# Sixteen more tokens by fetched expert rows, and a dense pass for 400 tokens in place of 416

## The chip, the core and the metric

The kernel runs on one core of a Trainium2 chip. The metric is the device time of one execution in microseconds (us), taken as the median of several runs. All data are fp32; products that need precision are made of three matmuls of split operands (high times high, high times low, low times high).

In the profile, PE is TensorE (its matmuls) and PEld its weight loads, DVE is VectorE, ACT is ScalarE, POOL is GpSimd, SP is SyncE, which issues most DMAs.

## The reference

One decoder layer for 576 tokens (512 of a prompt, 64 of eight running sequences): a mixer of windowed attention and a recurrent branch, then PEER, a layer of 16,384 experts, of which every token picks 16 in each of 8 heads. The change concerns PEER alone:

```python
def one(hc):
    c = hc.shape[0]
    q = (hc @ w_pq).reshape(c, PEER_HEADS, 2, D_KEY // 2)
    s = jnp.einsum('nhcd,hckd->nhck', q, sub_keys)
    sv, si = lax.top_k(s, PEER_TOPK)
    cand = (sv[:, :, 0, :, None] + sv[:, :, 1, None, :]).reshape(c, PEER_HEADS, -1)
    cid = (si[:, :, 0, :, None] * N_KEYS + si[:, :, 1, None, :]).reshape(c, PEER_HEADS, -1)
    best, pos = lax.top_k(cand, PEER_TOPK)
    eid = jnp.take_along_axis(cid, pos, axis=-1)
    g = jax.nn.softmax(best, axis=-1)
    act = jax.nn.gelu(jnp.einsum('nd,nhkd->nhk', hc, peer_u[eid]))
    return jnp.einsum('nhk,nhkd->nd', g * act, peer_v[eid])
```

`peer_u` and `peer_v` have 16,384 rows of 2,048 numbers each.

## The kernel before

Two ways of doing PEER run side by side.

**Dense.** The first `DEN` = 416 tokens are multiplied with all experts. `u_parts` (L741) makes the scores of one chunk of 128 experts: 16 blocks of 128 features, three matmuls each, with the weights loaded as the stationary operand and 416 token columns streamed (`mm3`, L96 to L99, tile `sps`). There are 128 chunks. The gelu of the scores goes to `e`; the first 40 chunks are put by in DRAM (`Ed`). The routing weights G of each token for each expert are built ahead (loop at L980 to L1008): for each token one product of two one-hot tiles (`pgg`, L1000), copied to a staging tile `stg` (ScalarE, L1002) and written to DRAM (`Gd`) in 13 groups of `GRP` = 32 tokens. Then come 16 groups of 8 chunks (`v_group`, L1159): `w_chunk` (L1147) multiplies `e` with G (tile `gs`, loaded from `Gd` by `load_g` and, for the next group, in pieces by L1170) and splits it, and 16 blocks of 24 matmuls make the output features (tile `po`), again with 416 columns; VectorE adds each block to `acc` (L1174). Between the groups run the score chunks of the next one. Weights arrive in pieces of 256 KB (`piece`, L75): a DMA issued on SP, a rounding on ScalarE (`phi`), a subtraction on VectorE (`plo`).

**Fetched.** The last 128 tokens lie one on each partition, and for each of their 128 expert slots the u row and the v row are fetched with an indirect DMA, in halves of 1,024 numbers for all 128 partitions at once, 512 KB a fetch (`fetch`, L1064, GpSimd's queue). VectorE makes the dot product (`gather_u`, L1072) or adds the scaled row (`gather_v`, L1078). 32 more tokens (`SPR`) are spread over four partitions each, so that each partition takes two heads of one token: 32 further slots. Their normalised rows are laid out by `spread_rows` (L765) through TensorE transposes (`ptx`) and DRAM (`hsd`), their routing results are put in place by small DMAs (`es`, L925), and at the end `spread_sum` (L1136) folds the four partitions of each token with 16 fp32 matmuls (`psum`). These are 160 slots, 640 fetches. `pace` (L1108) spreads them over the work: the dense part counts 464 units of 24 matmuls, and after unit 20 each unit may issue its share of the fetches, behind that unit's last split in VectorE's order.

Which experts the 128 tokens use is found by `gather_top` (L1031), eight heads of two small products (`psg`, "slot products" here) with top-16 searches on VectorE; one step of it is taken after each of the 16 blocks of the first V group.

A tile framework orders the instructions of each engine ahead of time from data dependencies and its own estimates; each engine then runs its queue in that order. `with tc.issue_after(ins)` makes the instructions that the block creates on the engine of `ins` stand behind it.

Of the kernel before, what the change touches and what calls it, by code (L numbers as in the profile page):

```python
# [8 lines left out]
F32 = mybir.dt.float32  # L9
# [17 lines left out]
DEN = 416  # L27
SPR = DQ - DEN
GRP = 32
BT = 8  # L30
NGRP = DEN // GRP
# [16 lines left out]
def tile_hymba_peer_step(ctx: ExitStack, tc: tile.TileContext, a, o, dbg=None):  # L48
# [47 lines left out]
    def mm3(out, sh, sl, mh, ml, first, last):  # L96
        pe.matmul(out, lhsT=sh, rhs=mh, start=first, stop=False)  # L97
        pe.matmul(out, lhsT=sh, rhs=ml, start=False, stop=False)  # L98
        pe.matmul(out, lhsT=sl, rhs=mh, start=False, stop=last)  # L99
# [27 lines left out]
    Gd = gd_pool.tile([NSG, P, NGRP, 8, GRP], F32, name="Gd")  # L127
# [517 lines left out]
    rt = per.tile([P, 5], F32, name="rt")  # L645
    es3 = per.tile([P, 3, SPR], F32, name="es3")
# [74 lines left out]
    def ffn_rstd():  # L721
# [10 lines left out]
        rsq(rt, pn[:, 0:5], 1.0 / D)  # L732
# [30 lines left out]
    hsd = gd_pool.tile([P, D], F32, name="hsd")  # L763

    def spread_rows(g4, pl):  # L765

        q = slice(g4 * 4, g4 * 4 + 4)
        t = pl.tile([P, 4, 4, SPR], F32, tag="sx", name="sx", bufs=2)
        dve.tensor_tensor(t, acc[:, q, None, DEN:].to_broadcast([P, 4, 4, SPR]),
                          gffn[:, q, None, None].to_broadcast([P, 4, 4, SPR]), op=ALU.mult)  # L770
# [4 lines left out]
        act.activation(r, pt.rearrange("p j n -> p (j n)"), AF.Copy, scale=rt[:, 4:5])  # L775
        sp.dma_start(hsd[:, g4 * 512:g4 * 512 + 512], r)
# [72 lines left out]
    with tc.tile_pool(name="tq", bufs=1) as tq:  # L849
# [35 lines left out]
        for h in range(8):  # L885
# [53 lines left out]
    with tc.tile_pool(name="gb", bufs=1) as gbp, tc.tile_pool(name="psg", bufs=2, space=PSUM) as psg:  # L939
# [37 lines left out]
        for r in range(NGRP):  # L977
# [6 lines left out]
            if g == 2 and t < 3:  # L984
                nxt = prep(t + 1)
# [327 lines left out]
```

## Time and profile before

| | us |
|---|---|
| median of 3 runs | 3421.17 (3417.39 to 3424.73) |
| the profiled execution | 3426.56 |
| its span, first to last instruction | 3424.8 |
| mean granted TensorE clock | 0.992 |
| busy PE / DVE / ACT / POOL | 3354.9 / 2535.3 / 1238.8 / 1229.3 |
| moved by DMA | 770.74 MB, 225 GB/s over the span |
| of it by fetches (GpSimd's queue) | 335.59 MB |

Busy times are sums over stages with different limits, and consecutive matmuls overlap in the profile, so TensorE's busy time is no measure of how fast it is fed. The table by stretch, the distance between matmul starts and the waits say more.

### The profile page before, as it was taken

To read this page: it belongs to the slowest core of one execution; us is meant where nothing else is said; L and a number is where in the kernel's file an instruction comes from. 1 tells how busy PE (TensorE), PEld (TensorE's weight loads), DVE (VectorE), ACT (ScalarE), POOL (GpSimd) and SP (SyncE) were. 2 spreads that over 40 slices of the span, in tenths; PEclk is the share of its full clock that TensorE was granted. 3 is DMA by queue.
4 is the path that set the end of the run, shared out by engine and by line. 5 is a ranking of instruction groups with operands and counts; after the bars stand their busy time and mean duration, and the time that the engine had idled before them with its cause. 6 is when DMAs were issued, how large, how long until landed. Compare 5 with 4: busy or idle time off the path is not lost.

```text
span 3424.8 us, 52637 instructions
## 1 busy us (share of the span) xinstructions
PE 3354.9 (98%) x18611; PEld 3220.6 (94%) x18611; DVE 2535.3 (74%) x4765; ACT 1238.8 (36%) x2127; POOL 1229.3 (36%) x1174
## 2 busy tenths in 40 slices
PE   9999999999999997999999999999999999999999
PEld 7887888889899997899999999999999999999999
DVE  5476655444759887888888887888878888888885
ACT  4245544333334443333333332333333333333332
POOL 6562231123642001434343333334333433443331
PEclk9999999999999999999999999999999999999999
DMA  4221223343334665789998888888888888988885
GB/s 146 81 63 55 67 63 111 99 142 110 92 97 137 204 223 183 284 290 332 334 315 291 300 297 300 300 294 298 292 307 303 287 309 295 316 306 289 307 290 193
DMA packets 364297, 770.74 MB, mean 225 GB/s; under 512 B 41184, under 2 KB 115552, under 8 KB 363744
## 3 DMA queue, kind: packets, MB, share of 16 engines
q1 hardware_dynamic: 266112, 423.26, 36.5%
q0 software_dynamic: 92160, 335.59, 29.2%
q10 hardware_dynamic: 5760, 8.52, 0.7%
q8 instruction: 147, 2.41, 0.3%
q14 instruction: 118, 0.97, 0.1%
HBM read 724.03 MB, written 45.11 MB: 225 GB/s over the span
## 4 chain that ended last, share of the span: by engine, by line
PE 88%; DVE 5%; DMA 2%; POOL 2%; issue 1%; ACT 1%; SPq 0%; ACTq 0%; DVEq 0%; POOLq 0%
PE po L99 11%; PE po L97 11%; PE po L98 11%; PE sps L99 10%; PE sps L97 10%; PE sps L98 10%; PE pgg L1000 3%; PE pd L99 2%; PE pd L98 2%; PE pd L97 2%; PE zp L97 2%; PE zp L98 1%; PE zp L99 1%; PE pdq L99 1%; PE mm L97 1%
## 5 line engine op out<-in xcount | busy, mean ns | idle before, releaser
L92 ACT ACTIVATE phi<-raw 128x512 fp32r<-128x512 f32 x1200 | 756.9, 632 | 1640.0 <-PE po L98 698.8
L93 DVE TENSOR_TENSOR plo<-raw,phi 128x512 fp32r<-128x512 f32 x1132 | 795.4, 704 | 283.9 <-ACT phi L92 266.1
L97 PE MATMUL po<-wth,phi 128*128 128x416 f32 x2048 | 719.7, 352 | 6.3 <-ACT wth L70 4.3
L99 PE MATMUL po<-wth,plo 128*128 128x416 f32 x2048 | 724.5, 354 | 0.0
L98 PE MATMUL po<-wtl,phi 128*128 128x416 f32 x2048 | 716.8, 350 | 0.6 <-DVE wtl L71 0.6
L1066 POOL DMA_INDIRECT row<-in_v,idx x320 | 396.1, 1238 | 605.0 <-DVE xg L1078 375.7
L1066 POOL DMA_INDIRECT row<-in_u,idx x320 | 388.6, 1214 | 589.8 <-DVE au L1072 465.3
L99 PE MATMUL sps<-uha,plo 128*128 128x416 f32 x1536 | 539.5, 351 | 5.9 <-DVE plo L93 3.3
L97 PE MATMUL sps<-uha,phi 128*128 128x416 f32 x1536 | 537.9, 350 | 1.2 <-DVE e L753 1.2
L98 PE MATMUL sps<-ula,phi 128*128 128x416 f32 x1536 | 537.5, 350 | 0.0
L97 PEld LDWEIGHTS po<-wth,phi 128*128 128x128 f32 x2048 | 385.6, 188 | 11.1 <-ACT wth L70 5.3
L98 PEld LDWEIGHTS po<-wtl,phi 128*128 128x128 f32 x2048 | 386.3, 189 | 8.2 <-DVE wtl L71 1.3
L99 PEld LDWEIGHTS po<-wth,plo 128*128 128x128 f32 x2048 | 385.5, 188 | 2.6
L1078 DVE SCALAR_TENSOR_TENSOR xg<-row,gg,xg 128x1024 f32<-128x1024 f32 x256 | 321.6, 1280 | 0.3
L1072 DVE CUSTOM_DVE_ANT_0 row<-row,hg 128x1024 f32<-128x1024 f32 x256 | 307.1, 1220 | 7.2 <-DMA row<-in_u,idx 7.2
L99 PEld LDWEIGHTS sps<-uha,plo 128*128 128x128 f32 x1536 | 289.0, 188 | 8.9 <-DVE plo L93 5.6
L97 PEld LDWEIGHTS sps<-uha,phi 128*128 128x128 f32 x1536 | 289.2, 188 | 1.7 <-ACT scs L860 1.4
L98 PEld LDWEIGHTS sps<-ula,phi 128*128 128x128 f32 x1536 | 289.0, 188 | 0.2
L1174 DVE TENSOR_TENSOR acc<-po,acc 128x416 f32<-128x416 f32 x256 | 150.8, 590 | 158.6 <-PE po L99 157.2
L99 PE MATMUL sps<-uhb,plo 128*128 128x416 f32 x512 | 181.3, 354 | 5.0 <-DVE plo L93 5.0
L98 PE MATMUL sps<-ulb,phi 128*128 128x416 f32 x512 | 180.2, 352 | 0.0
L97 PE MATMUL sps<-uhb,phi 128*128 128x416 f32 x512 | 180.1, 352 | 0.0
(427 smaller groups left out, 5316.9 us busy)
## 6 DMA issues: line engine op xcount, KB each, us to landing
raw<-in_uT SPq DMA_DIRECT2D x512, 256.0 KB
raw<-in_vL SPq DMA_DIRECT2D x512, 256.0 KB
Gd<-stg SPq DMA_DIRECT2D x13, 2048.0 KB
gs<-Gd SPq DMA_DIRECT2D x196, 128.0 KB
raw<-in_wlru SPq DMA_DIRECT2D x64, 256.0 KB
raw<-in_wout SPq DMA_DIRECT2D x64, 256.0 KB
raw<-in_wpq SPq DMA_DIRECT2D x64, 256.0 KB
raw<-in_wqkv SPq DMA_DIRECT2D x48, 256.0 KB
```

The lines of the kernel that those rows point to most:

```text
L92: act.activation(hi, raw, AF.Copy)
L93: ins = (pool if on_pool else dve).tensor_tensor(lo, raw, hi.bitcast(F32), op=ALU.subtract)
L97: pe.matmul(out, lhsT=sh, rhs=mh, start=first, stop=False)
L98: pe.matmul(out, lhsT=sh, rhs=ml, start=False, stop=False)
L99: pe.matmul(out, lhsT=sl, rhs=mh, start=False, stop=last)
L1000: pe.matmul(pg[:, k], lhsT=ohB[:, k], rhs=ohA[:, k].rearrange("p a b -> p (a b)"), start=True, stop=True)
L1066: pool.indirect_dma_start(out=r, out_offset=None, in_=uv[w], in_offset=bass.IndirectOffsetOnAxis(ap=idx2[:, half, e:e + 1], axis=0))
L1072: dve.tensor_tensor_reduce(r, r, rows[0][:, half * 1024:half * 1024 + 1024], 1.0, 0.0, ALU.mult, ALU.add, au[:, half, e:e + 1])
L1078: dve.scalar_tensor_tensor(xs, r, gg[:, e:e + 1], xs, op0=ALU.mult, op1=ALU.add)
L1174: dve.tensor_tensor(acc[:, b, 0:DEN], po, acc[:, b, 0:DEN], op=ALU.add)
```

## The change

48 tokens are now taken by spread rows, in two sets: the 32 tokens from 416 as before on four partitions each, and the 16 tokens from 400 on eight partitions each, one head of a token to a partition, 16 more slots. So there are 176 slots and 704 fetches, paced over the same units. The dense pass and the G build run for 400 tokens. The last group of G has 16 tokens (`REST`) and a DRAM tile of its own (`Gl`), and each multiplication with G is two instructions. The two sets share the tiles for normalised rows and for sums, one after the other: `next_h` loads the second set's rows late in the first, and `next_x` calls the fold of the first set (`spread_sum(0)`) early in the second. Last, each step of `gather_top` is put behind the last matmul of the block before it, in TensorE's order.

```diff
-DEN = 416
-SPR = DQ - DEN
+DEN = 400
+
+SETS = [(416, 32, 4), (400, 16, 8)]
-NGRP = DEN // GRP
+NGRP = -(-DEN // GRP)
+REST = DEN - (NGRP - 1) * GRP
...
-        for i in range(4):
-            pe.matmul(pn[i * SPR:i * SPR + SPR, 4:5], lhsT=ssd[:, DEN:DQ], rhs=ones[:, 0:1],
-                      start=True, stop=True)
+        for i, (n0, n, m) in enumerate(SETS):
+            sc = op.tile([P, P], F32, tag="gw", name="ssx")
+            dve.tensor_copy(sc.rearrange("p (m n) -> p m n", n=n), ssd[:, None, n0:n0 + n].to_broadcast([P, m, n]))
+            pe.matmul(pn[:, 4 + i:5 + i], lhsT=sc, rhs=ones[:, 0:1], start=True, stop=True)
...
-            if h in (1, 2):
-                for g4 in (2 * h - 2, 2 * h - 1):
-                    spread_rows(g4, tq)
+            if 1 <= h <= 4:
+                for g4 in range(2):
+                    spread_rows((h - 1) // 2, (h - 1) % 2 * 2 + g4, tq)
...
-        for g in range(4):
-            p0 = 64 * (g // 2) + SPR
-            sp.dma_start(es3[g * SPR:g * SPR + SPR], ei3[p0:p0 + SPR, :, (g % 2) * 32:(g % 2) * 32 + 32])
+        for (n0, n, m), es3 in zip(SETS, ess):
+            for g in range(m):
+                p0, k0 = 64 * (g * 2 // m) + n0 - 384, g % (m // 2) * n
+                sp.dma_start(es3[g * n:g * n + n], ei3[p0:p0 + n, :, k0:k0 + n])
...
-            sp.dma_start(Gd[:, :, r].rearrange("s p i n -> p s i n"),
+            sp.dma_start((Gd[:, :, r] if w == GRP else Gl).rearrange("s p i n -> p s i n"),
                          stg.rearrange("p (s i) n -> p s i n", i=8))
...
+    def next_x(i):
+        if i == 0:
+            sp.dma_start(o["yg"], rows[1])
+        else:
+            spread_sum(i - 1)
         rows[1] = per.tile([P, D], F32, tag="xg", name="xs")
         pool.memset(rows[1], 0.0)
...
     def load_g(s):
-        t = mn.tile([P, NGRP, 8, GRP], F32, tag="gs", name="gs")
-        for q in range(0, NGRP, 4):
-            q1 = min(q + 4, NGRP)
-            sp.dma_start(t[:, q:q1], Gd[s, :, q:q1])
+        t = g_tile()
+        for q in range(0, NGRP - 1, 4):
+            sp.dma_start(t[0][:, q:q + 4], Gd[s, :, q:q + 4])
+        load_part(t, s, NGRP - 1)
         return t
+
+    def g_tile():
+        t = mn.tile([P, 8 * DEN], F32, tag="gs", name="gs")
+        n = 8 * (DEN - REST)
+        return (t[:, 0:n].rearrange("p (g i n) -> p g i n", i=8, n=GRP),
+                t[:, n:].rearrange("p (i n) -> p i n", n=REST))
+
+    def load_part(t, s, b):
+        if b < NGRP - 1:
+            sp.dma_start(t[0][:, b], Gd[s, :, b])
+        else:
+            sp.dma_start(t[1], Gl[s])
...
-        ev = e.rearrange("p (g n) -> p g n", n=GRP)
-        dve.tensor_tensor(ev, ev, gs[:, :, c % 8, :], op=ALU.mult)
+        ev = e[:, 0:DEN - REST].rearrange("p (g n) -> p g n", n=GRP)
+        er = e[:, DEN - REST:]
+        dve.tensor_tensor(er, er, gs[1][:, c % 8], op=ALU.mult)
+        dve.tensor_tensor(ev, ev, gs[0][:, :, c % 8, :], op=ALU.mult)
...
             if s == 0:
-                next(top, None)
+
+                with tc.issue_after(done_mm[0].ins):
+                    next(top, None)
             if s == NSG - 1:
                 sp.dma_start(o["yT"][:, b, 0:DEN], acc[:, b, 0:DEN])
                 if b == NK - 2:
-                    spread_sum()
+                    spread_sum(len(SETS) - 1)
```

How the change moves instructions shows in the order of each engine's queue. TensorE, before, at the end of the G build (`sps` scores, `pgg` the build, `psg` a slot product, `po` a V block):

```order
L98 MATMUL sps<-ulb,phi 128x416
L99 MATMUL sps<-uhb,plo 128x416
L1000 MATMUL pgg<-ohA,ohB 128x128 x32
L1045 MATMUL psg__12698<-row 128x128 x2
L97 MATMUL po<-wth,phi 128x416 x2
L98 MATMUL po<-wtl,phi 128x416
L99 MATMUL po<-wth,plo 128x416
```

TensorE at the same place, after the change:

```order
L100 MATMUL sps<-ulb,phi 128x400
L101 MATMUL sps<-uhb,plo 128x400
L1009 MATMUL pgg<-ohA,ohB 128x128 x32
L99 MATMUL po<-wth,phi 128x400 x2
L100 MATMUL po<-wtl,phi 128x400
L101 MATMUL po<-wth,plo 128x400
```

The first slot product stood ahead of all `po` matmuls; now it stands behind the blocks, at this place further on in the queue:

```order
L99 MATMUL po<-wth,phi 128x400
L100 MATMUL po<-wtl,phi 128x400
L101 MATMUL po<-wth,plo 128x400
L1055 MATMUL psg__12733<-row 128x128 x2
L100 MATMUL po<-wtl,phi 128x400
L101 MATMUL po<-wth,plo 128x400
```

It moved from before the first block to behind the matmuls of a block. SP, before, at the same stage (`Gd` the routing weights written, `gs` the same read back, `qgd` and `skT` operands of slot products, `Ed` stored scores, `in_vL` weight pieces):

```order
L1007 DMA Gd<-stg 128x16x256
L80 DMA raw<-in_vL 128x512 x2
L1007 DMA Gd<-stg 128x16x256
L1123 DMA gs<-Gd 128x1024 x3
L1123 DMA gs<-Gd 128x256
L1041 DMA row<-qgd 128x256
L1042 DMA row<-in_skT 128x256
L1151 DMA e<-Ed_75 128x416
L1151 DMA e<-Ed_76 128x416
L1151 DMA e<-Ed_77 128x416
```

SP, after (`Gl` is the last group, `es` and `ei` routing results of the spread tokens):

```order
L1016 DMA Gd<-stg 128x16x256
L82 DMA raw<-in_vL 128x512 x3
L1016 DMA Gd<-stg 128x16x256
L1016 DMA Gl<-stg 128x16x128
L1141 DMA gs<-Gd 128x1024 x3
L1155 DMA gs<-Gl 128x128
L1051 DMA row<-qgd 128x256
L933 DMA es_5564<-ei_5565 16x3x16 x8
L1052 DMA row<-in_skT 128x256
L1189 DMA e<-Ed_76 128x400
```

The last write is half as long and its reading back a load of its own; eight small copies of the second set now stand between the loads of a slot product. VectorE, before, in front of the first V group (`e` and `gs` the gating, `wtl` the split of the gated scores, the L781 to L785 instructions the slot search):

```order
L1056 SCALAR_TENSOR_TENSOR row<-es_5562 128x32
L1153 TENSOR_TENSOR e<-e,gs 128x416 x3
L71 TENSOR_TENSOR wtl<-e,wth 128x416 x3
L781 MAX sv<-row 128x8 x2
L782 MAX_INDEX row<-sv,row 128x8
L783 MATCH_REPLACE s_12703<-sv,row 128x128
L782 MAX_INDEX row<-sv,row 128x8
L1153 TENSOR_TENSOR e<-e,gs 128x416
L784 MAX sv<-s_12703 128x8
L1153 TENSOR_TENSOR e<-e,gs 128x416
L785 MAX_INDEX row<-sv,s_12703 128x8
```

VectorE, after:

```order
L1069 SCALAR_TENSOR_TENSOR row<-es_5563 128x32
L1193 TENSOR_TENSOR e<-e,gs 128x384 x3
L1192 TENSOR_TENSOR e<-e,gs 128x16 x3
L73 TENSOR_TENSOR wtl<-e,wth 128x400 x2
L1069 SCALAR_TENSOR_TENSOR row<-es_5564 128x16
L1070 COPY gg<-es_5564 128x16
L73 TENSOR_TENSOR wtl<-e,wth 128x400
L1192 TENSOR_TENSOR e<-e,gs 128x16
L1193 TENSOR_TENSOR e<-e,gs 128x384
L1192 TENSOR_TENSOR e<-e,gs 128x16
L1193 TENSOR_TENSOR e<-e,gs 128x384
```

The search instructions that stood between the gating of the third and the fourth chunk are gone from there; each gating is two instructions.

## Rows read from the trace of the kernel before

**Rows 1.** Page, part 4: the chain that ended last, shares by engine.

```profile
PE 88%; DVE 5%; DMA 2%; POOL 2%; issue 1%; ACT 1%; SPq 0%; ACTq 0%; DVEq 0%; POOLq 0%
```

**Rows 2.** By stretch: length, busy PE, PEld, DVE, ACT, POOL, clock, DMA share, GB/s.

```profile
735.00:1075.00 340.00, 329.22 (x1893) 312.07 (x1894) 222.02 (x971) 122.88 (x211) 152.32 (x180) 0.99 0.34 102
1075.00:1290.00 215.00, 209.07 (x1459) 207.46 (x1457) 179.21 (x226) 93.41 (x121) 0.53 (x1) 1.00 0.63 202
1290.00:1400.00 110.00, 94.47 (x499) 92.04 (x500) 89.33 (x320) 36.16 (x62) 27.46 (x37) 0.93 0.55 172
1400.00:1800.00 400.00, 389.86 (x2032) 382.16 (x2032) 326.54 (x498) 129.33 (x218) 166.67 (x129) 0.99 0.92 324
1800.00:3410.00 1610.00, 1609.69 (x8562) 1600.55 (x8562) 1301.66 (x1944) 545.91 (x896) 615.12 (x508) 1.00 0.86 296
```

**Rows 3.** Timeline, TensorE: start us, length us, instruction. Widths 512, 288, 416.

```profile
99.64 0.39 PE L99 MATMUL mm<-phi,hl 128*128 128x512 f32 x1
...
101.70 0.40 PE L99 MATMUL mm<-phi,hl 128*128 128x512 f32 x1
...
439.72 0.30 PE L99 MATMUL zp<-hh,plo 128*128 128x288 f32 x1
...
441.98 0.29 PE L98 MATMUL zp<-hl,phi 128*128 128x288 f32 x1
...
2500.17 0.35 PE L98 MATMUL po<-wtl,phi 128*128 128x416 f32 x1
...
2511.88 0.35 PE L97 MATMUL po<-wth,phi 128*128 128x416 f32 x1
```

**Rows 4.** Groups by shape, TensorE: count | busy us, mean ns | idle before.

```profile
L97 PE MATMUL po<-wth,phi 128*128 128x416 f32 x2048 | 719.7, 352 | 6.3 <-ACT wth L70 4.3 <-DVE acc L1174 2.0
...
L97 PE MATMUL sps<-uha,phi 128*128 128x416 f32 x1536 | 537.9, 350 | 1.2 <-DVE e L753 1.2
...
L97 PEld LDWEIGHTS po<-wth,phi 128*128 128x128 f32 x2048 | 385.6, 188 | 11.1 <-ACT wth L70 5.3 <-DVE acc L1174 3.6
...
L97 PE MATMUL sps<-uhb,phi 128*128 128x416 f32 x512 | 180.1, 352 | 0.0
```

**Rows 5.** Chain in order of time (start us, us, what): G build and fold.

```profile
1097.44 3.57 PE pgg L1000 x32
...
3411.24 3.49 PE psum L1140 x32
```

**Rows 6.** The same view, end of the G build to the first V group.

```profile
1286.17 1.03 ACT stg L1002
1287.22 7.49 DMA Gd<-stg
...
1296.11 5.53 DMA gs<-Gd
1301.72 1.60 DVE e L1153 x3
...
1306.30 3.21 DMA row<-in_skT
```

**Rows 7.** Timeline, TensorE, the same place: slot product, first dense matmul; idle before.

```profile
1302.75 1.19 PE L1045 MATMUL psg__12698<-row 128*128 128x128 f32 x4 [16.62 <-DMA row<-in_skT]
...
1303.60 1.04 PE L97 MATMUL po<-wth,phi 128*128 128x416 f32 x2
```

**Rows 8.** Groups by shape, VectorE: products of fetched u and v rows.

```profile
L1078 DVE SCALAR_TENSOR_TENSOR xg<-row,gg,xg 128x1024 f32<-128x1024 f32 x256 | 321.6, 1280 | 0.3
L1072 DVE CUSTOM_DVE_ANT_0 row<-row,hg 128x1024 f32<-128x1024 f32 x256 | 307.1, 1220 | 7.2 <-DMA row<-in_u,idx 7.2
```

**Rows 9.** By stretch, columns as in rows 2: 10 us with full DMA queues.

```profile
1670.00:1680.00 10.00, 10.00 (x54) 9.91 (x53) 7.75 (x14) 3.17 (x5) 3.96 (x4) 1.00 1.04 395
```

**Rows 10.** Waits, 1390 to 1800: us in total, times, longest us.

```profile
DVE row L1072 <- DMA row<-in_u,idx: 7.2, 1, 7.2
```

**Rows 11.** Waits, 1800 to 3300, the same columns.

```profile
DVE e L1153 <- DMA gs<-Gd: 12.6, 6, 2.6
```

More of the change, by code (lines that the diff above doesn't have):

```diff
@@ L98, in mm3 @@
         pe.matmul(out, lhsT=sh, rhs=ml, start=False, stop=False)
-        pe.matmul(out, lhsT=sl, rhs=mh, start=False, stop=last)
+        return pe.matmul(out, lhsT=sl, rhs=mh, start=False, stop=last)
     def rsq(r, v, scale):
@@ L643, in tile_hymba_peer_step @@
     rd = per.tile([P, DQ], F32, name="rd")
-    rt = per.tile([P, 5], F32, name="rt")
-    es3 = per.tile([P, 3, SPR], F32, name="es3")
+    rt = per.tile([P, 6], F32, name="rt")
+    ess = [per.tile([P, 3, n], F32, name="es3") for _, n, _ in SETS]
     ei3 = per.tile([P, 3, 64], F32, name="ei3")
@@ L982, in tile_hymba_peer_step @@
             oa, ob = fac
+            w = GRP if r < NGRP - 1 else REST
             stg = gbp.tile([P, P, GRP], F32, tag="stg", name="stg", bufs=2)
+            stg = stg.rearrange("p i n -> p (i n)")[:, 0:P * w].rearrange("p (i n) -> p i n", n=w)
             if g == 2 and t < 3:
                 nxt = prep(t + 1)
-            for q in range(GRP // BT):
+            for q in range(w // BT):
                 n0 = g * GRP + q * BT
@@ L1018, in tile_hymba_peer_step @@
     uv = [a["u"].rearrange("e (t c) -> (e t) c", t=2), a["v"].rearrange("e (t c) -> (e t) c", t=2)]
[L1019 to L1021 removed]
+    NSL = P + sum(n for _, n, _ in SETS)
+    idx2 = mn.tile([P, 2, NSL], U32, name="idx2")
+    au = mn.tile([P, 2, NSL], F32, name="au")
+    gg = mn.tile([P, NSL], F32, name="gg")
     def row():
@@ L1084, in gather_act, with next_h @@
         dve.tensor_tensor(gg[:, e0:e0 + n], gg[:, e0:e0 + n], s, op=ALU.mult)
-    def next_h():
+    def next_h(i):
         rows[0] = per.tile([P, D], F32, tag="hg", name="hs")
-        sp.dma_start(rows[0], hsd)
-    def next_x():
-        sp.dma_start(o["yg"], rows[1])
+        sp.dma_start(rows[0], hsd[i])
+    def next_x(i):
[3 more added lines that the diff above has]
+            spread_sum(i - 1)
         rows[1] = per.tile([P, D], F32, tag="xg", name="xs")
         pool.memset(rows[1], 0.0)
-    jobs = []
-    for e0 in range(0, P + SPR, GE):
+    jobs, starts = [], [P]
+    for _, n, _ in SETS:
+        starts.append(starts[-1] + n)
+    for e0 in range(0, NSL, GE):
         u = [lambda e=e0 + k // 2, f=k % 2: gather_u(e, f) for k in range(2 * GE)]
@@ L1132, in v_half, with spread_sum @@
             k = q * 4 + d
[L1133 removed]
+            done_mm[0] = mm3(po, wh[:, d], wl[:, d], W[k][0], W[k][1], k == 0, k == 7)
         return ins
[L1136 to L1138 removed]
+    done_mm = [None]
+    def spread_sum(i):
+        n0, n, _ = SETS[i]
+        ps = pst.tile([P, NK, n], F32, tag="sg", name="psum", bufs=2)
         for b in range(NK):
[L1140 to L1145 removed]
+            pe.matmul(ps[:, b], lhsT=rows[1][:, b * P:b * P + P], rhs=sels[i], start=True, stop=True)
+        dve.tensor_tensor(acc[:, :, n0:n0 + n], ps, acc[:, :, n0:n0 + n], op=ALU.add)
+        if i == len(SETS) - 1:
+            sp.dma_start(o["yT"][:, :, DEN:], acc[:, :, DEN:])
+    sels = []
+    for _, n, _ in SETS:
+        sel = mn.tile([P, n], F32, name="sel")
+        dve.tensor_reduce(sel, ident.rearrange("p (g n) -> p n g", n=n), axis=AX.X, op=ALU.add)
+        sels.append(sel)
     def w_chunk(c, gs):
```

68 lines of the change are left out of this document (32 added, 36 removed).

## The prediction

> **What bounds the kernel now.** I read the chain of work that ended last first: TensorE carries 88% of it [rows 1], so an edit is worth what it takes from TensorE's queue, and everything else matters only where TensorE waits. Then the table by stretch [rows 2]: from 1800 to 3410 us TensorE is busy for 1609.7 of 1610 us at granted clock 1.00, while VectorE is busy 1301.7 (81%) and the DMA engines stand at a share of 0.86 with 296 GB/s. The stretches ahead of it have TensorE idle for 10.8 us (735 to 1075), 5.9 us (1075 to 1290), 15.5 us (1290 to 1400) and 10.1 us (1400 to 1800). So it is a TensorE-bound kernel with one real hole, at the hand-over from building G to the first V group.
>
> TensorE's busy time is not the price of a matmul, since consecutive ones overlap. The price is the distance between starts, and the timeline gives it: in a V group, with 416 columns, there are 62 steps from 2500.17 to 2511.88 us, 188.9 ns each [rows 3].
>
> **Dense pass, 416 to 400 columns.** What is streamed sets the step, as three widths show: 288 columns take 132.9 ns (2.26 us over 17 steps), 416 take 188.9, 512 take 228.9 (2.06 us over 9 steps) [rows 3]. From 288 to 512 that is 96.0/224 = 0.429 ns a column, so 16 columns are worth 6.86 ns. The dense pass has 2048 + 1536 + 512 matmuls of the first product [rows 4] and as many of each of the other two: 12,288. That is 12,288 x 6.86 ns = 84.3 us, all of it on the engine that sets the end. Bounds are the slopes of the two neighbouring pairs: 0.417 (416 to 512) gives 81.9 us, 0.4375 (288 to 416) gives 86.0.
>
> The Trainium skill, "TensorE: Matmul & The Clock Gate", section "Back-to-back issue gap", gives for a stream of weight loads and matmuls some 81 ns at 128 columns and 131 ns at 512, that is 0.13 ns a column: an estimate by it is 2.1 ns for 16 columns, 26 us in all instead of 84. It speaks against the change, and the trace does not bear it out here, since its 512-column step is 228.9 ns.
>
> **G build, 16 tokens less.** A token is one fp32 product, two matmul instructions; 32 of them take 3.57 us in a row [rows 5]. Sixteen tokens are 32 instructions: 3.6 us less on TensorE, in a stretch where it is busy 209 of 215 us [rows 2].
>
> **The hole between G and V.** The chain goes through DRAM [rows 6]: the last copy to the staging tile begins at 1286.17, its 2 MB write takes 7.49 us, the last of four loads back is issued 1.4 us later and lands after 5.53 us, then VectorE gates three score tiles. The first dense matmul starts at 1303.60 [rows 7], 17.4 us after that copy began. The slot product that stood first in TensorE's queue waited 16.62 us for its own load, but began only 0.85 us before the first dense matmul [rows 7], whose weights were not there earlier. Moving the slot products behind a block therefore frees some 0.85 us here by itself. More comes from the last group having 16 tokens: 1 MB to write, into a tile of its own, so that the three large loads no longer wait for it and only a 64 KB load does. If bytes set the write, 3.7 us are saved; if the number of runs does, which stays, nothing. The one small load saves 0 to 2.3 us (a slot load of 128 KB landed after 3.21 us [rows 6], against 5.53), and the issues ahead of it 1.4. Behind the hole TensorE loses another 1.9 us before 1400 (15.5 less the 13.6 from 1290 to 1303.6); slot work that stood between VectorE's gating operations now stands behind them. In all 1 to 10 us; I take 6, nearer the upper end because the two long pieces of the chain both shrink, and not higher because the large loads now share the queues with the last write. Eight small copies of routing results now stand on SP behind the loads of G, ahead of a slot load and the next score loads; those wait for score tiles that VectorE frees later, so I cost the copies at nothing. Without that cover they would cost TensorE 3.7 us, eight issues at the 0.47 us of the three just ahead of 1296.11.
>
> **What is added to TensorE.** A second fold of fetched sums, 32 instructions, 3.5 us [rows 5], in the last tenth of the program: it reads sums that VectorE has finished some five blocks earlier in its order, so it does not wait. Four more calls that spread token rows, 16 transposes in all at the fold's 0.11 us: 1.8 us. Both lie on the path.
>
> **What is added elsewhere.** 64 more fetches. On VectorE 32 x 1.220 + 32 x 1.280 us [rows 8] = 80 us, spread by the pacing over some 1,950 us, 4.1% of the time. With a TensorE that goes 3.8% faster, VectorE rises from 81% to 0.81 x 1.038 + 0.041 = 88%. It stays below TensorE. The other edits on VectorE (16 columns less on each dense operation, eight narrow multiplications more in a group) nearly cancel. GpSimd, which issues the fetches, is busy 615 of 1610 us [rows 2]; off the path. DMA: 64 x 512 KB = 33.6 MB, 17 GB/s, and the same traffic in less time, 296 x 1.038 = 307: about 325 GB/s, 330 with the busier early part. The queues can carry it: they moved 395 GB/s over 10 us with TensorE busy for all of them [rows 9].
>
> The four added row spreads stand at heads 3 and 4, where VectorE also resolves expert numbers; TensorE is idle 10.8 us in that stretch [rows 2]. Between nothing and a doubling of that I take +2, near nothing because the four calls of before stand in the same stretch. The first fetches: VectorE waited 7.2 us for the first row [rows 10] with splits for TensorE queued behind it, in the stretch where TensorE lost 10.1 us. Now the slot choice ends later against TensorE, some seven pieces further on in VectorE's order, and the fetches then run denser. Between -4 (a better place for the first wait) and +10 I take +3, nearest to nothing because the wait is of the same kind as now.
>
> **Sum.** -84.3 - 3.6 - 6 + 3.5 + 1.8 + 2 + 3 = -83.6 us. The profiled execution took 3426.56 us (span 3424.8 and 1.8 around it): 3343.0. It lies 0.16% above the median of the three runs, so the median becomes 3343.0 x 3421.17/3426.56 = 3337.7, say 3338. With all bounds at one end it is -98 or -60 us: 3323 to 3361.
>
> **Rivals.** (1) *Late loads at the group starts.* In each group the gating of the next weights needs the G load and the scores. It waited for G 12.6 us in six cases between 1800 and 3300, at most 2.6 us [rows 11], and buffered pieces hid that. If 10% more fetch traffic made TensorE see 2.6 us in each of 15 groups, that is 39 us: 3377. For it: a DMA share of 0.86 before. Against: TensorE idle for 0.3 us in all from 1800 to 3410, with that share [rows 2].
> (2) *The DMA queues cannot go above today's steady rate.* This is the slow end. From 1400 us on 400 x 324 and 1610 x 296 GB/s, 606 MB, are moved [rows 2]; with 33.6 more and 1.5 less for G and scores it is 638. If the early part keeps its rate and the rest stays at 296, it takes 400 + 508.7/0.296 = 2119 us in place of 2010: +109, less the 16 gained ahead of it. That is 3426.6 + 93 = 3520, median 3514. It decides as soon as the sustained rate is below some 330 GB/s, and at 313 the gain would be gone. Against it is [rows 9]; for it, that the table shows no such rate over hundreds of us. The Trainium skill, "DMA: Bandwidth & Descriptors", section "Specifications", puts the limit of one core's HBM at about 358 GB/s; the 10 us stretch lies above it and 330 would be below, so by that page too the queues would do.
> (3) *The weight load sets the step.* The rows of the 128x128 load last 188 ns, as long as the step [rows 4]. If the load were the limit, nothing of the 84.3 would come: 3343.0 + 84.3 = 3427, median 3422, no change. Against: at 288 columns the step is 132.9 ns with a load of the same size [rows 3].
> (4) *A slope a third as steep*: the three widths here would all have to mislead; 58 us worse, 3396. The page's figures above would have it so.
>
> **How the numbers follow.** Forecast 0.74; late loads 0.11 (3361 to 3400); DMA rate 0.06 (above 3428, slower); weight load 0.03 (no change); flatter slope 0.02; more than forecast, below 3323, 0.04. The range 3320 to 3372 holds the forecast's own and part of the late loads, and leaves out nearly 0.2. A measurement of this kernel tells apart about 0.2%, 7 us. Faster 0.91, same 0.03, slower 0.06.
>
> **What would show it.** Right: steps of the dense matmuls near 182 ns in the V groups; TensorE again busy for nearly all of the time after 1800; VectorE at 87 to 89%; DMA at 320 to 330 GB/s; 9 to 14 us from the start of the last staging copy to the first dense matmul; no wait ahead of the fold in mid-run. Wrong: TensorE waiting for splits whose raw piece or whose row came late (1, 2), or steps that stay above 185 ns (3, 4).

## The result, and the profile after

The changed kernel takes 3363.09 us (median of 4 runs, 3362.47 to 3365.34), the kernel before 3422.24: a ratio of 0.983 (95% interval 0.982 to 0.984). It is faster by 59 us, where 84 were forecast. The profiled execution took 3362.47 us, its span 3360.5.

The chain of work that ended last, as in [rows 1]:

```profile
PE 86%; DVE 7%; DMA 2%; POOL 2%; issue 1%; ACT 1%; SPq 0%; ACTq 0%; DVEq 0%; POOLq 0%
```

The stretches that answer [rows 2] (columns: length, busy PE, PEld, DVE, ACT, POOL, granted clock, DMA share, GB/s):

```profile
735.00:1075.00 340.00, 327.36 (x1898) 309.75 (x1898) 228.35 (x982) 127.31 (x219) 151.64 (x178) 1.00 0.35 105
1075.00:1280.00 205.00, 195.77 (x1390) 194.74 (x1389) 169.01 (x214) 89.00 (x113) 0.00 (x0) 0.99 0.66 209
1280.00:1390.00 110.00, 100.09 (x545) 98.61 (x546) 95.93 (x341) 40.01 (x69) 22.31 (x33) 0.94 0.54 168
1390.00:1790.00 400.00, 383.64 (x2053) 376.84 (x2052) 346.19 (x559) 129.18 (x216) 188.41 (x150) 0.98 0.97 345
1790.00:3350.00 1560.00, 1559.69 (x8565) 1559.30 (x8564) 1344.81 (x2090) 538.37 (x891) 694.74 (x557) 1.00 0.92 320
```

After 1790 us TensorE is busy all the time again, with 320 GB/s and VectorE at 86%. But from 1390 to 1790 it is idle for 16.4 us (10.1 before), and there the DMA share is 0.97 at 345 GB/s (0.92 and 324 before).

Where the time came from, by the starts of the first and last matmul of each stage in the two profiled executions. V0 to V15 are the sixteen V groups; V0 to V4 are called the first groups, those behind them the steady ones. `pdq` are the last products ahead of the G build. The forecast column gives each stage its share of the prediction's terms: 6.86 ns for each dense matmul in it, plus the terms that lie there.

| stage, to | before | after | difference in the stage | forecast |
|---|---|---|---|---|
| end of the mixer | 517.71 | 511.51 | -6.2 | 0 |
| last `pdq` (7 score chunks, row spreads) | 1021.72 | 1014.19 | -1.3 | +1.5 |
| last `pgg` (18 chunks, G build) | 1285.86 | 1271.59 | -6.7 | -9.5 |
| first `po` (the hole) | 1303.60 | 1288.10 | -1.2 | -6 |
| end of V0 | 1384.31 | 1366.30 | -2.5 | -2.6 |
| end of V4 | 1835.72 | 1812.48 | -5.2 | -12.8 |
| end of V13 | 3135.08 | 3073.62 | -38.2 | -47.4 |
| end of V14 (with the new fold) | 3279.45 | 3218.90 | +0.9 | -1.8 |
| end of V15 | 3420.55 | 3355.94 | -4.0 | -4.9 |

The first line is not the change's work: the same instructions run at another granted clock there, 0.96 before and 0.99 after from 180 to 440 us, and the end of the mixer lies anywhere between 511.5 and 517.3 us in the runs below. Without it the profiled gain is 58 us, and the misses are the steady groups (9 us), the first groups (8), the hole (5), the fold (3) and the G build (3), less 3 in the stage with the row spreads, which came out better.

**The steps.** The V step fell as forecast, from 188.9 ns [rows 3] to a mean of 181.7 (181.5 over the 46 steps between these two starts, one V block and most of the next):

```profile
2460.98 0.34 PE L99 MATMUL po<-wth,phi 128*128 128x400 f32 x1
...
2469.33 0.34 PE L100 MATMUL po<-wtl,phi 128*128 128x400 f32 x1
```

The score step did not. 33 steps of one score chunk before (first pair) take 6.16 us, 186.7 ns each; after (second pair) 6.05 us, 183.3 ns:

```profile
2151.79 0.35 PE L98 MATMUL sps<-ula,phi 128*128 128x416 f32 x1
...
2157.95 0.35 PE L98 MATMUL sps<-ula,phi 128*128 128x416 f32 x1
```

```profile
2119.48 0.35 PE L100 MATMUL sps<-ula,phi 128*128 128x400 f32 x1
...
2125.53 0.34 PE L100 MATMUL sps<-ula,phi 128*128 128x400 f32 x1
```

Over all steady chunks the mean goes from 187.1 to 183.2 ns. So the dense term is 6144 x 7.2 ns + 6144 x 3.9 ns = 68 us instead of 84.

**The hole.** The chain that answers [rows 6] (start, length, what):

```profile
1271.90 1.03 ACT stg L1011
1272.95 6.13 DMA Gl<-stg
...
1279.27 0.33 SPq L1141
...
1281.07 4.79 DMA row<-qgd
1285.86 1.48 DVE e L1193 x3
```

The last write is shorter (6.13 us, 7.49 before), but the three large loads of G (L1141) still start only when it has landed. SP's waits there (us in total, times, longest):

```profile
SPq L1141 <- DMA Gl<-stg: 5.8, 1, 5.8
```

TensorE begins 16.2 us after the start of the last staging copy, 17.4 before.

**The first groups.** Three stretches of 10 us at the start of V2, same columns as above:

```profile
1510.00:1520.00 10.00, 10.00 (x57) 9.92 (x55) 9.13 (x14) 4.18 (x8) 3.97 (x5) 1.00 1.03 399
1520.00:1530.00 10.00, 3.63 (x12) 2.38 (x10) 9.40 (x14) 1.00 (x3) 7.70 (x6) 0.74 0.99 361
1530.00:1540.00 10.00, 9.14 (x39) 8.47 (x39) 7.32 (x12) 3.34 (x6) 3.09 (x3) 0.75 0.95 318
```

TensorE loses some 7 us waiting for gated scores and then runs at a lower clock (0.74 and 0.75 in these stretches). Its wait in V2 (`wth` is the rounded half of the gated scores):

```profile
PE po L99 <- ACT wth L72: 7.1, 2, 6.1
```

V2 takes 80.8 us from its first to its last matmul; a steady group, which waits for nothing ("bare steps"), takes 69.6. V1 loses 7.6, V3 4.6, V4 3.0. Before, V1 lost 11 and V2 nothing.

**The fold.** It begins at 3170.33; the stretches are from before it to after it:

```profile
3160.00:3170.00 10.00, 10.00 (x57) 10.00 (x56) 8.59 (x15) 2.60 (x5) 4.80 (x4) 1.00 0.97 338
3170.00:3174.00 4.00, 4.00 (x35) 4.00 (x33) 2.55 (x5) 0.63 (x1) 2.26 (x3) 0.94 0.95 335
3174.00:3178.00 4.00, 4.00 (x16) 3.98 (x16) 0.97 (x2) 0.32 (x1) 1.85 (x2) 0.64 0.95 357
3178.00:3188.00 10.00, 10.00 (x56) 10.00 (x56) 8.32 (x15) 2.84 (x5) 3.55 (x3) 1.00 0.52 165
```

```profile
3170.33 3.98 PE L1174 MATMUL psum<-sel,xs 128*128 128x32 f32 x32
...
3174.60 0.54 PE L100 MATMUL po<-wtl,phi 128*128 128x400 f32 x1
3174.93 0.54 PE L101 MATMUL po<-wth,plo 128*128 128x400 f32 x1
```

After 3.8 us of matmuls with 32 columns the granted clock falls, and the dense steps behind the fold are 333 ns (1.2 GHz instead of 2.4) until some 3177. The fold costs 5.2 us in this execution, not 3.5.

It doesn't always do so. Of the twelve kernels run here with this fold, V14 takes 5.1 to 5.2 us more than its neighbours in four (the changed kernel, e4, e8 and e13 below) and 3.6 us in eight, where the clock stays at 1.00. This is e9, from 3.7 us after its fold began:

```profile
3175.50:3179.50 4.00, 4.00 (x23) 4.00 (x23) 2.18 (x4) 0.63 (x1) 3.55 (x3) 1.00 0.79 268
```

What decides between the two is open. The kernel before has a slow stretch of the same kind behind its only fold:

```profile
3411.08 3.65 PE L1140 MATMUL psum<-sel,xs 128*128 128x32 f32 x32
...
3415.57 0.55 PE L98 MATMUL po<-wtl,phi 128*128 128x416 f32 x1
3415.92 0.55 PE L99 MATMUL po<-wth,plo 128*128 128x416 f32 x1
```

Its V15, which holds the fold, takes 78.0 us, its V14 72.3.

### The profile page after: what moved, and what is told of

It is laid out like the page before. It is cut to its first block, busy times and chain, and to the rows that moved or that the text cites. A ratio compares the mean times of both kernels' runs of the same rounds, so it can differ in the third digit from the quotient of the medians.

```text
span 3360.5 us, 53163 instructions
## 1 busy us (share of the span) xinstructions
PE 3284.3 (98%) x18623; PEld 3162.3 (94%) x18623; DVE 2604.4 (78%) x4997; ACT 1235.5 (37%) x2130; POOL 1325.6 (39%) x1239
## 4 chain that ended last, share of the span: by engine, by line
PE 86%; DVE 7%; DMA 2%; POOL 2%; issue 1%; ACT 1%; SPq 0%; ACTq 0%; DVEq 0%; POOLq 0%
PE sps L101 11%; PE sps L100 10%; PE sps L99 10%; PE po L100 10%; PE po L101 10%; PE po L99 10%; PE pgg L1009 3%; PE pd L101 2%; PE pd L100 2%; PE pd L99 2%; PE zp L99 1%; PE zp L100 1%; PE zp L101 1%; DVE plo L95 1%; PE pdq L101 1%
## 5 line engine op out<-in xcount | busy, mean ns | idle before, releaser
L99 PE MATMUL po<-wth,phi 128*128 128x400 f32 x2048 | 706.3, 346 | 30.8 <-ACT wth L72 25.9
L100 PE MATMUL po<-wtl,phi 128*128 128x400 f32 x2048 | 709.8, 347 | 2.3 <-DVE wtl L73 2.2
L101 PE MATMUL po<-wth,plo 128*128 128x400 f32 x2048 | 709.4, 347 | 1.4 <-DVE plo L95 1.3
L101 PE MATMUL sps<-uha,plo 128*128 128x400 f32 x1536 | 531.8, 346 | 5.8 <-POOL plo L95 3.3
L99 PE MATMUL sps<-uha,phi 128*128 128x400 f32 x1536 | 530.8, 346 | 1.2 <-DVE e L757 1.2
L100 PE MATMUL sps<-ula,phi 128*128 128x400 f32 x1536 | 530.8, 346 | 0.0
L1214 DVE TENSOR_TENSOR acc<-po,acc 128x400 f32<-128x400 f32 x256 | 146.3, 572 | 123.1 <-PE po L101 121.4
L101 PE MATMUL sps<-uhb,plo 128*128 128x400 f32 x512 | 176.9, 346 | 1.2 <-DVE plo L95 1.2
L99 PE MATMUL sps<-uhb,phi 128*128 128x400 f32 x512 | 177.1, 346 | 0.0
L100 PE MATMUL sps<-ulb,phi 128*128 128x400 f32 x512 | 176.6, 345 | 0.0
```

The source lines that it names most:

```text
L101: return pe.matmul(out, lhsT=sl, rhs=mh, start=False, stop=last)
L1214: dve.tensor_tensor(acc[:, b, 0:DEN], po, acc[:, b, 0:DEN], op=ALU.add)
```

## The experiments

Each edit is to the changed kernel, and shown in part. "V2" and the like, with a time, are from the first to the last matmul of the group. All but the last kernel were run once, so their whole times are compared with the profiled execution of the changed kernel, 3362.47 us.

**Why the scores gained half (e1, e5, e10, e11).** First, other widths and start columns:

```diff
+CUT = [(0, 400), (8, 400), (16, 400), (24, 400), (0, 384), (0, 392), (0, 408), (0, 416), ...]
-                mm3(sps, wh[:, d], wl[:, d], uh[dk][:, 0:DEN], ul[dk][:, 0:DEN], dk == 0, dk == NK - 1)
+                c0, w = CUT[c % 12] if c >= NE else (0, DEN)
...
+                mm3(sps[:, 0:w], wh[:, d], wl[:, d], uh[dk][:, c0:c0 + w], ul[dk][:, c0:c0 + w],
+                    dk == 0, dk == NK - 1)
```

> The changed kernel with other streamed columns in the two dense products, so its sums are wrong from chunk 24 on; only the distance between matmul starts is read. In the scores, chunk by chunk in turn: 400 columns from column 0, 8, 16 and 24, and 384, 392, 408, 416, 424, 432, 448 and 352 columns from column 0. In the V blocks in turn: 400, 384, 392, 352 and 368 columns from 0, 384 from 8 and from 16, 392 from 8. Theory (where the streamed columns lie and how many they are sets a few ns on top of the columns): 400 columns from another start differ from the 183.1 ns by 2 ns or more in at least one case, and 384 and 352 columns come down to about 176 and 162 ns (0.43 ns a column). Rival (the weight load is a floor at about 182 ns for the scores): 352, 384 and 392 columns all stay at 181 ns or more, and the start column changes nothing.

Mean steps in the first twelve feature blocks, about 290 each, from the starts in the timeline:

| columns from 0 | 352 | 384 | 392 | 400 | 408 | 416 | 424 | 432 | 448 |
|---|---|---|---|---|---|---|---|---|---|
| ns | 160.2 | 176.6 | 178.8 | 180.5 | 186.8 | 186.8 | 186.8 | 193.7 | 202.2 |

400 columns from 8 take 183.1, from 16 180.2, from 24 180.1 (right behind a chunk from 16). In the blocks of the steady V groups, from column 0, 352 columns take 161.3, 384 174.0, 400 181.8. So there is no floor (352 gives 160), and the steps are a staircase: 408, 416 and 424 cost the same. But 400 from 0 takes 180.5 here (180.0 in the chunks between steady groups alone) and 183.3 in the changed kernel, so something else takes part.

```diff
+    if row % 4 == 2:
+        return 0, 352 if (c - 1) % 8 == 2 else DEN
+    return (16 if row % 4 == 3 else 8), DEN
```

> The changed kernel with other streamed columns in some score chunks (its sums are wrong there; only the distance between matmul starts is read). The eight chunks between two V groups make a row; the rows change in turn: all 400 columns from column 0; the same with a 352-column chunk in third place; all 400 from column 16; all 400 from column 8. In the kernel with mixed widths 400 columns from 0, 16 and 24 took 180.1 to 180.5 ns in the first twelve feature blocks and 400 from 8 took 183.3, though in the changed kernel all chunks, 400 from 0, take 183.1. Theory A (what ran just before decides which rhythm the engine falls into): in the second kind of row the chunks ahead of the narrow one take 183 ns and the ones behind it 180 to 181; the rows from 0, 16 and 8 look alike at their start. Theory B (the place of the columns decides): rows from 16 take 180 to 181 throughout, rows from 0 and from 8 take 183, and the narrow chunk changes nothing behind it.

Rows from 0 and from 8: 183.2 to 183.4 ns in every chunk. Rows from 16: 180.1 to 180.3 in every chunk, from the first one behind a V group on. In the mixed rows the one chunk behind the narrow one runs at 180.0, the next at 183.3 again. One pair of starts, 33 steps apart, for a row from 16 and one for a row from 0:

```profile
2106.58 0.34 PE L111 MATMUL sps<-ula,phi 128*128 128x400 f32 x1
...
2112.52 0.34 PE L111 MATMUL sps<-ula,phi 128*128 128x400 f32 x1
...
2385.84 0.35 PE L111 MATMUL sps<-ula,phi 128*128 128x400 f32 x1
...
2391.89 0.34 PE L111 MATMUL sps<-ula,phi 128*128 128x400 f32 x1
```

So the place decides (theory B), and theory A holds for one chunk, which explains the 180.5 of 400 from 0 in the mixed kernel: there it always followed a narrow chunk. The next kernel moves the operands themselves (its first line also parts the two tiles of routing results, as e4 below does):

```diff
-    ess = [per.tile([P, 3, n], F32, name="es3") for _, n, _ in SETS]
+    ess = [per.tile([P, 3, n], F32, tag=f"es{n}", name="es3") for _, n, _ in SETS]
...
+    h2b.tile([P, 16], F32, name="pad")
     uhb = h2b.tile([P, NK - NA, DQ], F32R, name="uhb")
...
     gg = mn.tile([P, NSL], F32, name="gg")
+    mn.tile([P, 48], F32, name="pad")
```

> The changed kernel with the operands of the scores moved in memory and nothing else of them changed: the first twelve feature blocks 192 bytes down, the last four 64 bytes up, so that their first column lies 96 and 160 bytes above a multiple of 256, as columns from 16 did; the pads also part the two tiles of routing results. Theory (the place of the streamed columns sets the rhythm of the scores): 180 to 180.6 ns a step in the scores instead of 183.2, about 6144 x 3 ns = 18 us less in all, nearly all of it after V3: 3343 to 3348 us. Rival (it was the column number within the tile, or something else that moved with it, not the address): 183 ns as before and 3358 to 3364 us.

```profile
2115.03 0.34 PE L100 MATMUL sps<-ula,phi 128*128 128x400 f32 x1
...
2120.97 0.34 PE L100 MATMUL sps<-ula,phi 128*128 128x400 f32 x1
```

180.0 ns, and 3345.11 us. The time falls evenly, 1.1 us in each row of eight chunks. So it is an address that counts, not the column number within the tile. Of the 17 us, 3 lie in V14 and V15, where the clock did not fall behind the folds in this execution. The same for the V blocks (two small tiles moved to make room):

```diff
-        wth = mn.tile([P, DEN], F32R, tag="wth", name="wth", bufs=8)
-        wtl = mn.tile([P, DEN], F32R, tag="wtl", name="wtl", bufs=8)
+        wth, wtl = [mn.tile([P, DQ], F32R, tag=t, name=t, bufs=8)[:, 0:DEN] for t in ("wth", "wtl")]
```

> The changed kernel with the sixteen tiles of gated scores 1792 bytes apart instead of 1600, each beginning 96 bytes above a multiple of 256 (at 1600 they take four places in turn). Theory (the same rhythm holds in the V blocks, whose steps of 176 to 188 ns have a mean of 181.7): steps near 180 ns, 6144 x 1.7 ns = 10 us less. Rival (the V blocks have their own reasons, as the weight tiles change with every matmul pair in the scores too): a mean within 0.7 ns of 181.7 and the time within 4 us.

```profile
2458.58 0.34 PE L99 MATMUL po<-wth,phi 128*128 128x400 f32 x1
...
2466.86 0.34 PE L100 MATMUL po<-wtl,phi 128*128 128x400 f32 x1
```

46 steps of 180.0 ns, and 3350.50 us, with a mixer that ended 4.9 us later than in the changed kernel: the gain behind it is 17 us, of which 10 are V steps and 3 the folds, as in e10. Most of the rest is in the scores, whose operands this edit left where they were: the last four feature blocks of a steady chunk fall from 183.5 to 180.4 ns a step, while the first twelve stay at 183.3. What moved for those four blocks is the buffer that holds their weights, from 160 to 32 bytes above a multiple of 256 in the built program. So the address of the streamed operand does not decide alone; that of the weights takes part.

Put together, with the bytes above a multiple of 256 of the streamed operand and of the weights, the steps of 400 columns in the scores are:

| streamed / weights | 32 / 96 | 64 / 96 | 96 / 160 | 128 / 160 | 96 / 96 | 160 / 160 | 96 / 32 |
|---|---|---|---|---|---|---|---|
| ns | 183.3 | 183.2 | 183.5 | 183.4 | 180.1 | 180.5 | 180.4 |
| run | changed | e5 | changed | e5 | e5, e10 | e5, e10 | e11 |

The fast ones are those in which the streamed operand lies as far above as the weights, or farther. This is a reading of seven pairs that no run was made to test, and it is for 400 columns: in the kernel before, with 416, 32 / 96 takes 186.7 and 96 / 96 188.8 ns.

**What the parts cost (e2, e3, e4).**

```diff
-                with tc.issue_after(done_mm[0].ins):
-                    next(top, None)
+                next(top, None)
```

> The changed kernel without the last part of the change: the steps of the slot choice are no longer put behind the block before them. Theory (the place of the slot products is worth about a microsecond at the hole and nothing later): the first V block starts 0.5 to 1.5 us later, the end of V1 is within 3 us of the changed kernel's 1479.28, and the stall in V2 (80.8 us from its first to its last matmul where V4 takes 72.6) stays above 5 us. Rival (the new order pushes the slot choice and the first fetches late, and VectorE has the backlog in V2): V2 comes down to below 75 us.

3375.64 us. V0 begins 0.34 us later against the last G product, takes 3.1 more, V3 2.8 more, and by the end of V4 8.8 us are lost. V2 still takes 82.1 us, so the rival falls; but the theory's "nothing later" falls too. In V0 TensorE now waits for a slot operand, with the blocks queued behind it (waits: us in total, times, longest):

```profile
PE psg__12799 L1055 <- DMA row<-in_skT: 2.7, 1, 2.7
```

```diff
     state = [0, 0]
+    jobs = jobs[:640]
...
-                    spread_sum(len(SETS) - 1)
+                    spread_sum(0)
```

> The changed kernel without the 64 fetches and the fold of the second set (16 tokens lack their fetched sum), the other 640 fetches spread over the same units as before the change. Theory (10% more fetched rows leave VectorE a backlog at the start of V2 and V3): V2 takes 73 us or less from first to last matmul instead of 80.8, V3 72.6 instead of 74.2, and from V4 on everything is as in the changed kernel except for the 5.2 us of the fold. Rival (the faster TensorE alone brings the gating too late): V2 stays above 77 us.

3351.15 us. V2 77.9, V3 70.3, V4 71.7, and 5.2 us less in V14. So the 64 fetches cost 7.6 us from the end of V1 to the end of V4 (6.6 counted from the first matmul of V0) and nothing visible in the steady groups; the fold, in the execution with the slow clock, costs 5.2. V2 went as the rival had it, V3 further than the theory.

```diff
-    ess = [per.tile([P, 3, n], F32, name="es3") for _, n, _ in SETS]
+    ess = [per.tile([P, 3, 32], F32, name="es3"), rd[:, DEN:].rearrange("p (w n) -> p w n", n=16)]
```

> The changed kernel with the routing results of the second set in memory of their own (the unused last 48 columns of another tile at unchanged addresses), so that their eight small copies don't wait for VectorE to have read the first set's and move ahead of the G build's end. Theory (the eight copies on SP hold up the score loads behind them): the first matmul of V0 moves by less than 1 us, but the time from the last G product to the last matmul of V0 falls from 94.7 to 89 to 91 us. Rival (the return of G sets the whole hole): it stays above 93.5 us.

3361.80 us, and 94.8 us from the last G product to the end of V0: the rival holds. SP's issues in that place, the copies now gone from it:

```profile
1280.91 1.28 SPq L1141 DMA_DIRECT2D gs<-Gd  x3
...
1283.39 0.46 SPq L1052 DMA_DIRECT2D row<-in_skT  x1
1290.74 6.16 SPq L1189 DMA_DIRECT2D e<-Ed  x5
```

The score loads wait on SP from 1283.9 to 1290.7 for the tiles that VectorE has to free. The copies were hidden behind that.

**What stalls V1 to V3 (e7, e8, e9, e13).**

```diff
-        want = min(len(jobs), max(0, state[0] - UNIT0) * len(jobs) // (UNITS - UNIT0 - 4) + 1)
+        n, m = state[0] - UNIT0, UNITS - UNIT0 - 4
+        want = min(len(jobs), max(0, n if n < 54 else 54 + (n - 54) * (len(jobs) - 54) // (m - 54)) + 1)
```

> The changed kernel with the fetches paced more slowly at first: one a unit for 54 units (to the start of V3) instead of 1.6, and 1.68 a unit after that. Theory (VectorE comes out of the slot choice late and then has too many fetched rows in front of the gating of V1 to V3): from the first matmul of V1 to that of V4, 337.9 us in the changed kernel against 314 us of bare steps, it takes 328 us or less, nothing is lost after V4, and the time is 3350 to 3355 us. Rival (the stalls of V1 to V3 are the dense work's own, fetches or not): 334 us or more there, and the time stays within 4 us of 3363.

3355.33 us, with a mixer that ended 2.6 us later than in the changed kernel; 325.1 us from V1 to V4, as the theory had it. V2 is free of stalls (this stretch is nearly all of it), V4 loses 3 us more, nothing is lost later:

```profile
1516.00:1586.00 70.00, 70.00 (x387) 69.99 (x386) 54.25 (x80) 23.56 (x41) 17.64 (x17) 1.00 0.84 285
```

Fewer fetches take away both VectorE's products and bytes. Three more kernels follow. e8 and e13 take work from VectorE and leave the fetches; e9 spreads the slot choice over two groups and starts the fetches later.

```diff
-        wh, wl, ins = piece(a["vL"][s, b, :, q * 4:q * 4 + 4], [P, 4, P], False)
+        wh, wl, ins = piece(a["vL"][s, b, :, q * 4:q * 4 + 4], [P, 4, P], s < 3 and q == 0 and b % 2 == 0)
```

> The changed kernel with the weight subtraction of every fourth piece in V0, V1 and V2 (8 a group) done by GpSimd (1.3 us each) instead of VectorE (0.6 us each); fetches and their bytes as before. Theory (VectorE's queue sets V0 to V2): from the first matmul of V0 to that of V3, 342.3 us in the changed kernel, it takes 4 to 12 us less. Rival (the DMA queues, whose share is 0.95 to 1.0 there, set it): within 2 us of 342.3, or more because GpSimd issues the fetches later.

3369.53 us; 346.2 us from V0 to V3, worse. TensorE waited for subtractions at the start of V0 (2.4 us, 1.3 in the changed kernel). GpSimd takes 1.31 us for a subtraction where VectorE takes 0.70 (means in the kernel before), which may be why, but this isn't shown; so this run says little on VectorE.

```diff
-UNIT0 = 20
+UNIT0 = 34
...
-            if s == 0:
+            if s < 2 and b % 2 == 0:
```

> The changed kernel with one step of the slot choice behind every second block of V0 and V1, instead of behind every block of V0, and the fetches begun 14 units later, 1.65 a unit instead of 1.6. Theory (VectorE's work is heaped up in V0 to V2, and there is room for it later): from the first matmul of V0 to that of V4, 451.8 us in the changed kernel against 419 us of bare steps, it takes 437 us or less, nothing is lost after V4, and the time is 3345 to 3352 us. Rival (the slot choice, done later, only moves the same stalls to V1 to V3): 447 us or more.

3356.88 us; 444.5 us from V0 to V4, between the two expectations. V0 is no shorter (79.0), V1 and V2 are, by 6.0 and 5.4 us: counted from the first matmul of V0, the first fetch comes 7 us later and the first product of a fetched row 43 us later. Inconclusive on the slot choice, but it again helps where fetches are fewer.

```diff
+        if state[1] < 114:
+            dve.tensor_copy(au[:, half, e:e + 1], r[:, 0:1])
+            return
         dve.tensor_tensor_reduce(r, r, rows[0][:, half * 1024:half * 1024 + 1024], 1.0, 0.0,
```

> The changed kernel in which the first 114 fetched rows (those up to the end of V3) are still fetched, in the same order and pace, but VectorE reads one number of each instead of making the product, so the fetched sums are wrong. This parts the two things that fewer fetches take away together. Theory (VectorE's products stand in front of the gating): from the first matmul of V1 to that of V4 it takes 325 us or less, as with the slower pace (325.1) or better, where the changed kernel takes 337.9. Rival (the bytes of the fetches keep the weight pieces and scores back): 334 us or more.

3358.93 us; 332.3 us, nearer to the rival. V2 still takes 78.4 us, with VectorE at little more than half:

```profile
1511.00:1521.00 10.00, 8.82 (x49) 8.49 (x47) 6.11 (x17) 3.82 (x7) 5.56 (x6) 1.00 1.04 400
1521.00:1531.00 10.00, 7.04 (x24) 5.95 (x25) 5.48 (x14) 2.87 (x5) 2.60 (x4) 0.66 1.04 402
```

VectorE's timeline there (idle time before an instruction and what ended it in brackets): it waits for a fetched row, with the gating queued behind, and then for the stored scores.

```profile
1521.54 0.22 DVE L1097 SCALAR_TENSOR_TENSOR xg<-row,gg,xg 128x1 f32<-128x1 f32 x1 [1.85 <-DMA row<-in_v,idx]
...
1523.81 0.18 DVE L1197 TENSOR_TENSOR e<-e,gs 128x16 f32<-128x16 f32 x1 [1.02 <-DMA e<-Ed]
```

So of the 23 us that V1 to V3 lose, VectorE's products, all taken away, account for 5.6, give or take some 2: in e4 and e5, which leave the fetches as they are, the same stretch takes 336.3 and 339.2 us. The slower pace, which leaves many products but has fewer bytes too, gave back 12.7. If the two effects add, some 7 of it are the bytes: at about 400 GB/s the queues are full (share 1.04), and rows and scores come late. That is a difference of two runs; no run takes away the bytes alone. How much of the other 10 us is the dense work's own stays open.

**All three together (e12).** The score operands 64 bytes up (by a shorter `rd` above them), the gated scores as in e11, the slower first pace:

```diff
-    rd = per.tile([P, DQ], F32, name="rd")
+    rd = per.tile([P, 432], F32, name="rd")
...
+        early = min(n, 54) + max(0, min(n, 78) - 54) * 13 // 10
+        want = min(len(jobs), early + max(0, n - 78) * (len(jobs) - 85) // (m - 78) + 1)
```

> The changed kernel with three things: the operands of the first twelve feature blocks 64 bytes up (96 above a multiple of 256), the tiles of gated scores 1792 bytes apart at 96 above a multiple of 256, and the fetches paced one a unit to the start of V3, 1.3 to the end of V4 and 1.71 after that. If the three add: 18 us (place of the score operands), 10 us (place of the gated scores) and 8 us (pace) less than 3363, so 3325 to 3330 us. Rival (with TensorE 1.4% faster and the pace denser after V4, VectorE, at some 90%, becomes late in the steady groups): stalls in V5 to V14 and 3335 us or more.

3325.47 us (4 runs, 3325.28 to 3326.20), a ratio of 0.972 to the kernel before (95% interval 0.970 to 0.973) and 38 us below the changed kernel. The gains add up:

```profile
1400.00:1800.00 400.00, 391.98 (x2149) 390.43 (x2149) 318.72 (x524) 132.37 (x223) 140.24 (x116) 0.99 0.89 308
1800.00:3320.00 1520.00, 1519.70 (x8456) 1519.07 (x8454) 1360.08 (x2116) 527.59 (x879) 734.92 (x585) 1.00 0.95 337
```

TensorE is idle for 8 us instead of 16 in the first groups, with 308 GB/s there, and still for nothing later, with VectorE at 89% and 337 GB/s.

## Why the prediction was right in direction and its gain 25 us too large

In the prediction's own terms: the dense pass gave 68 us instead of 84 and the hole 1 instead of 6; the first groups lost 9 instead of 3 and the fold 5 instead of 3.5; the row spreads and their stage, put at 3.8, cost nothing that shows; the G build gave its 3.6. Part of it is luck: 3363 us lies beyond 3361, where the sum ends with all its bounds at one end, and inside the stated range only by the part added for late loads, which the prediction itself gave 0.11.

- **What bounds the kernel** was right: an edit is worth what it takes from TensorE's queue, and fetches paced over the steady groups cost nothing there (e3).
- **The dense term was mis-sized**: 68 us, not 84. The V half came as forecast (7.2 ns against 6.86). The step that failed is the line through 288, 416 and 512 columns: two of those widths came from mixer products with other operands, the third from a V block alone, and the price of a column was taken as smooth and the same for the scores. It is a staircase on which the operands' addresses take part. At the score operands' addresses 416 columns were cheap (186.7 ns, 188.9 in the V blocks) and 400 dear (183.3 ns, 180.0 at the addresses of e10). The bounds 81.9 to 86.0, from neighbouring pairs of three widths, could not hold this.
- **The weight load as floor (rival 3) and the flat slope (rival 4)** are out: 352 columns take 160 ns, and between 352 and 448 a column costs 0.44 ns. The slope that I worked out from the Trainium skill, "TensorE: Matmul & The Clock Gate", section "Back-to-back issue gap", does not hold here.
- **The hole was mis-sized**: 1.2 us at the first matmul, not 6, and 16.2 us from the last staging copy, where 9 to 14 were said. The step that failed is "the three large loads no longer wait" for the last write: they do (5.8 us on SP), although it has a tile of its own. The wait is part of the program: ahead of the first of these loads the framework has put one on the semaphore that the last write raises. In e11 the tile they fill lies clear of the staging tiles and they still wait (issued at 1284.24, the write issued at 1277.93). A kernel in which they don't wait was not tried; why the framework puts the wait there is open. Costing the eight copies at nothing was right, with the reason given (e4).
- **Putting the slot products behind the block** was costed at 0.85 us; it is worth 8.8 by the end of V4 (e2). Without it the first groups would have gained nothing at all: from the first matmul of V0 to the last of V4, e2 takes 532.9 us and the kernel before 532.1.
- **The first fetches were mis-sized**: +3 with a range to +10; the first groups ended 7.6 us worse than forecast, 1.8 of it from the dense term, so the fetches' term came to some +9. Rival 2 held there in small: the queues did not go far above 400 GB/s (no 10 us stretch of any run passes 415), and I had read 395 GB/s over 10 us [rows 9] as room, while it was close to the ceiling. It did not hold for the steady groups, at 320 and, in e12, 337 GB/s over 1520 us. The Trainium skill, "DMA: Bandwidth & Descriptors", section "Specifications", puts a core's HBM limit at about 358 GB/s. The traces go above it: 399 to 402 in 10 us stretches, and 366 over 200 us in e13 (1397 to 1597).
- **The fold**: 5.2 us instead of 3.5 in this execution, for the clock behind it, and 3.6, as forecast, in eight of twelve. The trace of before had both prices: 3.49 us for the instructions [rows 5], and 5.7 us by which its V15 with the fold is longer than V14. **G build** as forecast but for the score steps in it; the row spreads cost less than the 3.8 forecast: that stage gained 1.3 us, as much as its 336 score steps x 3.9 ns give.
- **The mixer** gave 6.2 us in this pair of executions that the change has no part in; the median, too, compares such executions.

## What to carry to other kernels

Measure the step of a matmul stream at the width and at the addresses it will have, rather than taking a slope from other products; a shift of 64 bytes was worth as much as seven columns here. When transfers are paced over a program, pace them against each stretch's own demand: a share of 1.0 over 10 us is a ceiling reached, and what waits behind it can show up as a late operand on another engine. A short run of narrow matmuls in a dense stream costs its own length and, in four of the twelve kernels here, a slow stretch behind it; price it from an execution that shows the steps behind it.

## What was not expected of the hardware

- 400-column fp32r matmuls (the split operands' type) follow each other at 183.3 or 180.0 ns by the addresses of their operands: for the first twelve feature blocks, with weights 96 bytes above a multiple of 256, a streamed operand 32 and 64 bytes above one was slow, 96 fast. For the last four, 96 was slow with weights at 160 and fast with weights at 32. Why is open. A faster rhythm set by a narrower chunk lasts for one chunk.
- 408, 416 and 424 columns take the same 186.8 ns at the score operands' addresses (e1).
- 3.8 us of 32-column matmuls between dense ones brought the granted clock down to 0.64 in the next 4 us of the changed kernel; in eight of twelve kernels it stayed at 1.00 behind the same fold.
